# The FFN's remaining GpSimd work goes to VectorE, and sums of the sample's down weights are kept in place

## The chip, the cores and the metric

The kernel runs on one core of a Trainium2 chip. The metric is device time in microseconds of one execution; lower is better.

## The reference

One layer of an encoder with 1024 features, for a prompt of 512 rows and a sample of 1024 rows, in fp32: RMSNorm, an input projection, differential attention beside a recurrent branch, an output projection with residual, then the part that matters here:

```
h2 = rmsnorm(x, norm_ffn)
x  = x + (silu(h2 @ w_gate) * (h2 @ w_up)) @ w_down     # d_ff = 2816
y  = rmsnorm(x, norm_final)
```

## The kernel before

**Split products.** Activations lie feature-major, a page being 128 features by 512 rows. Every fp32 operand of a product is split into a high part (ScalarE casts it to fp32r) and a low part (the operand less its high part, one subtraction of two SBUF tiles). A product is three matmuls a tile: high by high, low by high, high by low (`mm3`, lines 222 to 224). `split` (lines 150 and 151) does the split; `Part.put` (682, 683) does it for a part of the activations, `weight_parts` (713, 714) for FFN weights.

**Stages.** After the prompt's gate and up products and the sample's attention come, in this order:

1. The sample's output projection, then the prompt's low half of the down product (`low_parts` with `down`, 22 steps of 12 matmuls). Beside it `token_parts` normalises the sample's two blocks of 512 rows and forms the parts of the activations that the next stage multiplies. It forms eight sums of 128x1024 by `minus` (line 691).
2. The sample's gate and up (`gate_up`). It treats the two row blocks and the weights as 2 by 2 blocks and does seven products in place of eight (Strassen's scheme in Winograd's form). Each of 11 steps j does gate and up in turn, and each of these forms four sums of weights of 128x512 (lines 706 and 691), splits seven weight parts and multiplies. At the end of a step come the activation, four more sums (`put_sample`, on VectorE already) and seven stores from ScalarE's queue.
3. The sample's down product (`sample_parts`), seven products q = 0 to 6 of 11 steps each, 12 matmuls a step. The weights stay in SBUF as low pages (a11, a12) and high pages (a21, a22). For q = 2 to 5 the weight operand is a sum, made anew in each step in a buffer of the ring "mh", in part on VectorE and in part on GpSimd as FORMS_S says.
4. The prompt's high half of the down product, and the final norms.

**Where GpSimd works.** `minus` has GpSimd as its default; line 706 names it; the low weight split of every third step of `low_parts` goes there (POOL_E); of the sums in stage 3 five instructions a step are its own (one each for q = 2, 3, 4, two for q = 5). Two products in the very last norm are on it in both kernels.

**What sets the order.** Each engine runs its own queue in order. The queues are laid down when the program is built; generators such as `advance` and `Ring` (a look-ahead of five products, LOOK and LOOK2) say which work is put beside which, and a planner places each instruction on its engine's queue when it expects its operands, so that a queue isn't strictly in the order of the code. Loads go out on SP's queue; a raw weight page has three buffers ("raw"), split weights have six ("w").

Of the kernel before, what the change touches and what calls it, by code (L numbers as in the profile page):

```python
# [11 lines left out]
F32 = mybir.dt.float32  # L12
# [4 lines left out]
ALU = mybir.AluOpType  # L17
# [3 lines left out]
P = 128  # L21
# [21 lines left out]
N_RAW, AHEAD, LOOK, LOOK2, LOOK3, LOOK4, LATE = 3, 2, 5, 4, 4, 4, 2  # L43
# [7 lines left out]
SKEW = (0, 1)  # L51
WARM = 16
YG = 0.6
POOL_X = (3,6)

POOL_P = (1, 3, 5)
POOL_S = ()
POOL_E = (0,)
POOL_Q = ()
FORMS_T = (0, 0, 0, 0)  # L60
FORMS_S = (0, 1, 1, 1, 0, 1, 1)
HP_RINGS = ("raw",) * 3 + ("pg",) * 3


# [20 lines left out]
def drain(gen):  # L85
    for _ in gen:
        pass


def build(tc, io, es):  # L90
    nc = tc.nc
    V, A, T = nc.vector, nc.scalar, nc.tensor
    VG = (nc.vector, nc.gpsimd)

    def pool(stack, name, bufs=1, **kw):
        return stack.enter_context(tc.tile_pool(name=name, bufs=bufs, **kw))
# [5 lines left out]
    rings = {}  # L102
# [46 lines left out]
    def split(h, l, src, eng=V):  # L149
        A.copy(h, src)  # L150
        eng.tensor_tensor(l, src, h.bitcast(F32), ALU.subtract)  # L151
# [520 lines left out]
    class Part:  # L672
# [5 lines left out]
        def put(self, src, eng=None):  # L678

            n = 2 * BLK // self.w  # L680
            h, l = (rings[self.ring]([P, n, self.w], self.name + i, F32R) for i in "hl")
            A.copy(h, src)
            (eng or V).tensor_tensor(l, src, h.bitcast(F32), ALU.subtract)
            self.h += [h[:, q] for q in range(n)]
            self.l += [l[:, q] for q in range(n)]

    def parts_of(rs, w):
        return [Part(f"b{i}{w}", r, w) for i, r in enumerate(rs)]

    def minus(out, a, b, eng=nc.gpsimd):  # L690
        eng.tensor_tensor(out, a, b, ALU.subtract)

    def weight_parts(pooled, early=()):

        for j in range(NP):
            for name in ("w_gate", "w_up"):
                r = []
                for f in (j, j + NP):
                    r.append(rings["raw"]([P, KC, P], "wr"))
                    nc.sync.dma_start(r[-1], io[name][f].rearrange("p (k m) -> p k m", k=KC))  # L700
                a11, a12, a21, a22 = (x[:, k:k + 4] for x in r for k in (0, 4))
                s1, s2, s3 = (rings[q]((P, 4, P), f"s{i}") for i, q in enumerate(early or ("mh",) * 3))
                early = ()
                for i, src in enumerate((a11, s2, a12, s3, s1, a22, s2)):
                    if i == 1:
                        nc.gpsimd.tensor_tensor(s1, a21, a22, ALU.add)
                        minus(s2, s1, a11)
                    elif i == 3:
                        minus(s3, a11, a21)
                    elif i == 6:  # L710
                        minus(s2, a12, s2)
                    h = rings["w"]((P, 2, 4, P), "ws", F32R)
                    A.copy(h[:, 0], src)  # L713
                    (nc.gpsimd if i in pooled else V).tensor_tensor(h[:, 1], src, h[:, 0].bitcast(F32), ALU.subtract)
                    yield h[:, 0], h[:, 1]

    def product(out, w, act, first):
# [5 lines left out]
    def pair_products(res, ws, acts, tag, uring, keep):  # L723

        B11, B12, B21, B22, T1, T2, T3, T4 = acts
        n = B11.w
        cost = (3 * ((4 - 1) % FINE + 1)) * n / 2400
        if keep:
            x, y, z = (bank(i, t) for i, t in zip("xyz", tag))
        else:  # L730

            xz, y = bank("xz", tag), bank("y", tag)[:, 0:n]
            x, z = xz[:, 0:n], xz[:, n:2 * n]
        u = rings[uring]([P, 2, n], "u")
        u2, u3 = u[:, 0], u[:, 1]
        e = rings["mh"]([P, 1 if keep else 2, n], "e")
        e, e2 = e[:, 0], e[:, 0 if keep else 1]
        yield from product(x, next(ws), B11, True)
        A.copy(e, x)
        yield cost  # L740
        yield from product(y, next(ws), T2, True)
        V.tensor_tensor(u2, y, e, ALU.add)
        yield cost
        yield from product(x, next(ws), B21, False)
        if not keep:
            A.copy(e2, x)
        yield cost
        yield from product(y, next(ws), T3, False)
        V.tensor_tensor(u3, y, e, ALU.add)
        yield cost  # L750
        yield from product(z, next(ws), T1, True)
        yield cost
        yield from product(y, next(ws), T4, False)
        V.tensor_tensor(u3, z, u3, ALU.add)
        V.tensor_tensor(e, y, e, ALU.add)
        yield cost
        yield from product(z, next(ws), B22, False)
        V.tensor_tensor(u2, z, u2, ALU.add)
        res += [x if keep else e2, u2, e, u3]
        yield cost  # L760

    def gate_up(ws, acts, put, tags, rs, keep):

        n = acts[0].w
        uring, tring = rs
        for j in range(NP):
            gs, us, four = [], [], []
            yield from pair_products(gs, ws, acts, tags[0], uring, keep)
            yield from pair_products(us, ws, acts, tags[1], uring, keep)
            for g, u in zip(gs, us):  # L770
                t = rings[tring]([P, n], "t")
                A.activation(t, g, AF.Tanh, scale=0.5)
                V.scalar_tensor_tensor(t, t, 1.0, g, ALU.add, ALU.mult)
                V.tensor_tensor(t, t, u, ALU.mult)
                four.append(t)
            put(j, four)
# [23 lines left out]
    def low_parts():  # L800

        for f in range(NF):
            hr = rings["xh"](HALF, "hr")
            nc.sync.dma_start(hr, hid[f])
            hp = [rings["mh"](HALF, "hp", F32R) for _ in range(2)]
            split(*hp, hr)
            wr = rings["raw"]([P, KC, P], "wr")[:, 0:4]
            nc.sync.dma_start(wr, io["w_down"][f][:, 0:BLK].rearrange("p (k m) -> p k m", k=4))
            w = rings["w"]((P, 2, 4, P), "ws", F32R)
            split(w[:, 0], w[:, 1], wr, VG[f % 3 in POOL_E])  # L810
            yield (w[:, 0], w[:, 1]), hp

    def down(parts, n, acc, new):
# [115 lines left out]
    b11, b21, b22, t4, t1, t2, t3 = parts_of(["main"] * 4 + ["pg"] * 3, BLK)  # L929
# [50 lines left out]
    def put_sample(j, four):  # L980
        f11, f12, f21, f22 = four
        t1, t2, t4 = (rings["sums"](HALF, f"ht{i}") for i in range(3))
        minus(t1, f12, f11, VG[FORMS_T[0]])
        minus(t2, f22, t1, VG[FORMS_T[1]])
        minus(f12, f22, f12, VG[FORMS_T[2]])
        minus(t4, f21, t2, VG[FORMS_T[3]])
        for q, t in enumerate((f11, f21, t2, t1, f12, f22, t4)):
            nc.scalar.dma_start(hid_s[q][j], t)

    parts = Ring(weight_parts(POOL_S), LOOK)  # L990
    parts.fill()
    drain(gate_up(parts, (b11, None, b21, b22, t1, t2, t3, t4), put_sample, (("aux", "aux", "pv"), ("mm",) * 3), ("pg", "xh"), True))

    low, high = [], []
# [41 lines left out]
    def pair(ring):  # L1039
        w = rings[ring]((P, 2, 4, P), "ws", F32R)  # L1040
        return w[:, 0], w[:, 1]
# [6 lines left out]
    def sample_parts():  # L1048
        loads = Ring(sample_loads(), LOOK4)
        for q in range(7):  # L1050
            for j in range(NP):
                loads.fill()
                a11, a12, a21, a22 = low[j][:, 0], low[j][:, 1], high[j][:, 0] if q else None, high[j][:, 1] if q else None
                if q in (0, 1, 6):
                    src = (a11, a12, a22)[min(q, 2)]
                else:
                    src = rings["mh"]((P, 4, P), "s")
                    if q == 2:
                        VG[FORMS_S[0]].tensor_tensor(src, a21, a22, ALU.add)
                        minus(src, src, a11, VG[FORMS_S[1]])  # L1060
                    elif q == 3:
                        VG[FORMS_S[2]].tensor_tensor(src, a21, a22, ALU.add)
                    elif q == 4:
                        minus(src, a11, a21, VG[FORMS_S[3]])
                    else:
                        VG[FORMS_S[4]].tensor_tensor(src, a11, a12, ALU.add)
                        minus(src, src, a21, VG[FORMS_S[5]])
                        minus(src, src, a22, VG[FORMS_S[6]])
                w = pair("w")
                split(*w, src, VG[q in POOL_Q])  # L1070
                hr = next(loads)
                hp = page()
                split(hp[:, 0], hp[:, 1], hr)
                yield w, (hp[:, 0], hp[:, 1])
# [76 lines left out]
    parts = Ring(sample_parts(), LOOK2)  # L1151
# [83 lines left out]
```

## Time and profile before

| | us |
|---|---|
| median of 3 runs | 1801.11 |
| lowest, highest | 1796.82, 1801.77 |
| the profiled execution's own time | 1798.27 |
| its span, first to last instruction | 1796.5 |

| engine | busy us | share |
|---|---|---|
| TensorE (PE) | 1743.1 | 97% |
| VectorE (DVE) | 1331.4 | 74% |
| ScalarE (ACT) | 827.2 | 46% |
| GpSimd (POOL) | 256.5 | 14% |

Times in the profile's views are microseconds from the span's start. The granted clock of TensorE was 0.989 of full speed over the span. A matmul in flight overlaps the next, so TensorE's busy time can stay near full while fewer matmuls start; their count in a stretch tells more.

### The profile page before, as it was taken

What the parts mean: (1) busy time and instruction counts of PE and PEld (TensorE: products, weight loads), DVE (VectorE), ACT (ScalarE), POOL (GpSimd) and SP (SyncE); (2) the same over time, 40 slices, a digit from 0 to 9 for tenths busy, and PEclk for the clock granted to TensorE, in tenths of its full rate; (3) what the DMA queues carried; (4) which work ended last, traced back from release to release, by engine and by line L of the source; (5) the groups of instructions that cost most, each with busy time, mean ns of one, the idle gap of its engine ahead of it and who ended that gap; (6) DMA issues with size and microseconds to landing.
All of it is one profiled execution on the core that took longest, in us unless ns stands there. A gap on an engine that the chain in (4) does not pass through costs nothing.

```text
span 1796.5 us, 22898 instructions
## 1 busy us (share of the span) xinstructions
PE 1743.1 (97%) x8316; PEld 1434.9 (80%) x8316; DVE 1331.4 (74%) x2154; ACT 827.2 (46%) x1327; POOL 256.5 (14%) x165
## 2 busy tenths in 40 slices
PE   8999999999999999999999979999999999998997
PEld 7777787777888888888788768888888888887797
DVE  6789878777587778786544996767766766989884
ACT  6568556665355545554323432332233334444451
POOL 0000000000000000000000362323322310555200
PEclk9999999999999999999999989999999999999998
DMA  8633424153473222222555642223332239532361
GB/s 291 198 102 111 142 87 135 66 179 119 145 218 114 86 89 93 70 88 71 196 167 180 205 142 100 100 94 106 110 108 100 100 122 369 170 112 70 99 207 54
DMA packets 105026, 238.79 MB, mean 133 GB/s; under 512 B 12240, under 2 KB 21200, under 8 KB 104912
## 3 DMA queue, kind: packets, MB, share of 16 engines
q1 hardware_dynamic: 76608, 185.04, 32.3%
q10 hardware_dynamic: 28304, 52.28, 7.6%
q8 instruction: 65, 1.06, 0.2%
q14 instruction: 49, 0.40, 0.1%
HBM read 180.00 MB, written 57.28 MB: 132 GB/s over the span
## 4 chain that ended last, share of the span: by engine, by line
PE 79%; DVE 10%; ACT 4%; issue 3%; DMA 3%; POOL 1%; ACTq 0%; SPq 0%; DVEq 0%; POOLq 0%
PE gu L222 5%; PE gu L224 4%; PE gu L223 4%; PE pm L223 4%; PE pm L222 4%; PE pm L224 4%; PE acc L223 3%; PE acc L222 3%; PE acc L224 3%; PE y L224 3%; PE y L222 3%; PE y L223 3%; PE sc L591 2%; PE po L223 2%; PE sc L592 2%
## 5 line engine op out<-in xcount | busy, mean ns | idle before, releaser
L222 PE MATMUL pm<-xh,wh 128*128 128x512 f32 x480 | 189.9, 396 | 5.7 <-ACT wh L209 3.3
L223 PE MATMUL pm<-xl,wh 128*128 128x512 f32 x480 | 189.2, 394 | 1.1 <-DVE xl L336 1.1
L224 PE MATMUL pm<-xh,wl 128*128 128x512 f32 x480 | 189.1, 394 | 0.3 <-DVE wl L210 0.3
L209 ACT CAST wh<-wr 128x1024 fp32r<-128x1024 f32 x100 | 104.8, 1048 | 148.5 <-PE gu L223 62.4
L151 POOL TENSOR_TENSOR ws<-wr,ws 128x512 fp32r<-128x512 f32 x8 | 12.7, 1582 | 1013.2 <-ACT ws L150 1013.2
L223 PE MATMUL acc<-hp,ws 128*128 128x512 f32 (+1 forms) x396 | 142.8, 361 | 6.3 <-DVE hp L151 6.3
L222 PE MATMUL acc<-hp,ws 128*128 128x512 f32 (+1 forms) x396 | 143.2, 362 | 2.8 <-ACT hp L150 2.8
L224 PE MATMUL acc<-hp,ws 128*128 128x512 f32 (+1 forms) x396 | 142.5, 360 | 0.6 <-DVE ws L151 0.6
L222 PE MATMUL gu<-yh,wh 128*128 128x512 f32 x352 | 142.0, 403 | 0.9 <-DVE ev L384 0.9
L224 PE MATMUL gu<-yh,wl 128*128 128x512 f32 x352 | 139.0, 395 | 0.0
L223 PE MATMUL gu<-yl,wh 128*128 128x512 f32 x352 | 138.6, 394 | 0.0
L210 DVE TENSOR_TENSOR wl<-wr,wh 128x1024 fp32r<-128x1024 f32 x100 | 122.2, 1222 | 17.6 <-ACT wh L209 16.9
L597 ACT ACTIVATE pb<-pb,mn 128x1024 f32<-128x1024 f32 (+1 forms) x96 | 96.9, 1009 | 73.5 <-DVE mn L594 73.4
L151 DVE TENSOR_TENSOR hp<-hr,hp 128x512 fp32r<-128x512 f32 (+1 forms) x143 | 111.0, 787 | 26.3 <-ACT hp L150 22.4
L594 DVE CUSTOM_DVE_ANT_0 pb<-sc,tab 128x1024 f32<-128x1024 f32 (+1 forms) x96 | 100.1, 1043 | 33.1 <-PE sc L592 31.6
L713 ACT CAST ws<-s 128x512 fp32r<-128x512 f32 x88 | 54.7, 622 | 131.1 <-PE y L224 48.1
L222 PEld LDWEIGHTS pm<-xh,wh 128*128 128x128 f32 x480 | 90.6, 189 | 24.5 <-ACT wh L209 3.5
L150 ACT CAST hp<-hr 128x512 fp32r<-128x512 f32 (+1 forms) x143 | 77.2, 550 | 71.0 <-PE acc L224 24.1
L223 PEld LDWEIGHTS pm<-xl,wh 128*128 128x128 f32 x480 | 90.5, 189 | 19.8 <-DVE xl L336 1.8
L224 PEld LDWEIGHTS pm<-xh,wl 128*128 128x128 f32 x480 | 90.6, 189 | 19.4 <-DVE wl L210 1.0
L713 ACT CAST ws<-wr 128x512 fp32r<-128x512 f32 x66 | 41.1, 622 | 111.1 <-PE y L224 38.2
L223 PEld LDWEIGHTS acc<-hp,ws 128*128 128x128 f32 x396 | 76.3, 193 | 18.1 <-DVE hp L151 7.4
(271 smaller groups left out, 4604.6 us busy)
## 6 DMA issues: line engine op xcount, KB each, us to landing
wr<-w_gate SPq DMA_DIRECT2D x44, 512.0 KB, 3.5
wr<-w_up SPq DMA_DIRECT2D x44, 512.0 KB, 3.5
wr<-w_in SPq DMA_DIRECT2D x40, 512.0 KB, 4.1
hr<-hs SPq DMA_DIRECT2D x77, 256.0 KB, 2.8
hs<-t ACTq DMA_DIRECT2D x44, 256.0 KB, 2.0
hs<-ht ACTq DMA_DIRECT2D x33, 256.0 KB, 2.9
wr<-w_out SPq DMA_DIRECT2D x16, 512.0 KB, 3.6
xd<-xh ACTq DMA_DIRECT2D x28, 256.0 KB, 2.5
```

The source lines that it names most:

```text
L150: A.copy(h, src)
L151: eng.tensor_tensor(l, src, h.bitcast(F32), ALU.subtract)
L209: A.copy(h, r)
L210: V.tensor_tensor(l, r, h.bitcast(F32), ALU.subtract)
L222: T.matmul(out, lhsT=wh, rhs=ah, start=first, stop=False, skip_group_check=more)
L223: T.matmul(out, lhsT=wh, rhs=al, start=False, stop=False, skip_group_check=more)
L224: T.matmul(out, lhsT=wl, rhs=ah, start=False, stop=last, skip_group_check=more)
L591: T.matmul(sc[:, w], lhsT=qh[m][:, qs], rhs=K[m][:, w], start=True, stop=False)
L592: T.matmul(sc[:, w], lhsT=ql[m][:, qs], rhs=K[m][:, w], start=False, stop=True)
L594: V.tensor_tensor_reduce(out=pp[m], in0=sc, in1=tab[:, 896 - q0:896 - q0 + n], scale=-0.125, scalar=3e38, op0=ALU.add, op1=ALU.min, accum_ ...
L597: A.activation(pp[m], pp[m], AF.Exp, scale=-1.0, bias=mn, accum_out=zz)
L713: A.copy(h[:, 0], src)
```

## The change

All FFN sums and splits that GpSimd did are issued on VectorE: the eight sums in `token_parts`, the low splits of `low_parts`, four sums of weights for each gate or up of a step. In the sample's down product the sums are kept: at q = 1 the page a11 is overwritten by a11 - a21, at q = 4 a12 by a12 - a22 and at q = 5 a12 by a12 + a11, so that q = 4 and q = 5 need no buffer of their own, and each of q = 1 to 5 has one sum a step.

```diff
-    def minus(out, a, b, eng=nc.gpsimd):
-        eng.tensor_tensor(out, a, b, ALU.subtract)
+    def minus(out, a, b):
+        V.tensor_tensor(out, a, b, ALU.subtract)
...
-                        nc.gpsimd.tensor_tensor(s1, a21, a22, ALU.add)
+                        V.tensor_tensor(s1, a21, a22, ALU.add)
...
-            split(w[:, 0], w[:, 1], wr, VG[f % 3 in POOL_E])
+            split(w[:, 0], w[:, 1], wr)
...
-                if q in (0, 1, 6):
-                    src = (a11, a12, a22)[min(q, 2)]
-                else:
-                    src = rings["mh"]((P, 4, P), "s")
-                    if q == 2:
-                        VG[FORMS_S[0]].tensor_tensor(src, a21, a22, ALU.add)
-                        minus(src, src, a11, VG[FORMS_S[1]])
-                    elif q == 3:
-                        VG[FORMS_S[2]].tensor_tensor(src, a21, a22, ALU.add)
-                    elif q == 4:
-                        minus(src, a11, a21, VG[FORMS_S[3]])
-                    else:
-                        VG[FORMS_S[4]].tensor_tensor(src, a11, a12, ALU.add)
-                        minus(src, src, a21, VG[FORMS_S[5]])
-                        minus(src, src, a22, VG[FORMS_S[6]])
+                if q == 1:
+                    minus(a11, a11, a21)
+                src = None
+                if q in (2, 3):
                     src = rings["mh"]((P, 4, P), "s")
+                if q == 2:
+                    minus(src, a22, a11)
+                elif q == 3:
+                    V.tensor_tensor(src, a21, a22, ALU.add)
+                elif q == 5:
+                    V.tensor_tensor(a12, a12, a11, ALU.add)
+                if src is None:
+                    src = a11 if q in (0, 4) else a12 if q in (1, 5) else a22
                 w = pair("w")
-                split(*w, src, VG[q in POOL_Q])
+                split(*w, src)
+                if q == 4:
+                    minus(a12, a12, a22)
```

## Rows read from the trace of the kernel before

**Rows 1.** The page: TensorE's busy time; VectorE and GpSimd in 40 slices, tenths.

```profile
PE 1743.1 (97%) x8316; PEld 1434.9 (80%) x8316; DVE 1331.4 (74%) x2154; ACT 827.2 (46%) x1327; POOL 256.5 (14%) x165
...
DVE  6789878777587778786544996767766766989884
...
POOL 0000000000000000000000362323322310555200
```

**Rows 2.** By stretch: length, PE, PEld, DVE, ACT, POOL busy (instructions), clock, DMA, GB/s.

```profile
1016.20:1061.40 45.20, 39.68 (x164) 31.88 (x163) 42.74 (x32) 19.93 (x28) 32.56 (x14) 0.92 0.41 128
1025.00:1050.00 25.00, 20.28 (x80) 16.15 (x79) 25.00 (x18) 12.64 (x19) 15.58 (x6) 0.86 0.40 118
1050.00:1075.00 25.00, 20.41 (x74) 15.54 (x73) 22.84 (x18) 8.44 (x14) 18.65 (x9) 0.86 0.47 166
1075.00:1100.00 25.00, 25.00 (x112) 20.70 (x111) 14.90 (x22) 8.33 (x15) 6.74 (x5) 1.00 0.22 72
1076.00:1474.00 398.00, 396.77 (x1739) 325.24 (x1738) 275.25 (x372) 122.58 (x209) 118.96 (x81) 1.00 0.29 99
1650.00:1675.00 25.00, 16.93 (x61) 12.91 (x61) 21.79 (x26) 12.75 (x24) 15.52 (x10) 0.86 0.23 63
1675.00:1700.00 25.00, 23.48 (x101) 18.74 (x102) 22.41 (x49) 13.26 (x25) 0.00 (x0) 0.93 0.32 100
```

**Rows 3.** TensorE's waits from 975 to 1700 us: total, times, longest.

```profile
PE acc L223 <- DVE hp L151: 6.3, 3, 3.0
PE sc L223 <- DVE hp L151: 4.7, 1, 4.7
```

**Rows 4.** The order of time in the sample's down product: start, duration, instruction.

```profile
1634.70 0.68 DVE L1066 TENSOR_TENSOR s<-wlo 128x512 f32<-128x512 f32 x1
1635.30 0.68 DVE L151 TENSOR_TENSOR ws<-s,ws 128x512 fp32r<-128x512 f32 x1
1635.51 3.32 POOL L691 TENSOR_TENSOR s<-s,whi 128x512 f32<-128x512 f32 x2 [1.29 <-issue]
1635.90 1.79 DVE L151 TENSOR_TENSOR hp<-hr,hp 128x512 fp32r<-128x512 f32 x1
1637.61 1.77 DVE L151 TENSOR_TENSOR ws<-whi,ws 128x512 fp32r<-128x512 f32 x1
```

**Rows 5.** VectorE's groups, 1498 to 1526 and 1016.2 to 1061.4 us: busy, mean ns | idle.

```profile
L151 DVE TENSOR_TENSOR hp<-hr,hp 128x512 fp32r<-128x512 f32 x12 | 8.2, 686 | 3.0 <-ACT hp L150 3.0
...
L659 DVE SCALAR_TENSOR_TENSOR y<-y,par,bc 128x512 f32<-128x512 f32 x8 | 5.4, 744 | 0.2 <-PE bc L271 0.2
L683 DVE TENSOR_TENSOR b4512l<-y,b4512h 128x1024 fp32r<-128x1024 f32 x2 | 2.4, 1213 | 0.0
```

**Rows 6.** The order of time around 990 us, VectorE and TensorE.

```profile
987.49 1.22 DVE L260 TENSOR_TENSOR rtm<-rsm 128x4 f32<-128x4 f32 x1
...
989.66 0.15 DVE L260 TENSOR_TENSOR rtm<-rsm 128x4 f32<-128x4 f32 x1
...
991.27 0.68 PE L271 MATMUL bc<-dg,onesq 128*128 128x128 f32 x4 [3.97 <-DVE dg L270]
```

**Rows 7.** VectorE's groups in the sample's gate and up, 1076 to 1474 us.

```profile
L714 DVE TENSOR_TENSOR ws<-s,ws 128x512 fp32r<-128x512 f32 x82 | 63.1, 769 | 21.1 <-ACT ws L713 19.6
...
L773 DVE SCALAR_TENSOR_TENSOR t<-t,u 128x512 f32<-128x512 f32 x22 | 24.8, 1127 | 0.0
L774 DVE TENSOR_TENSOR t<-t,e 128x512 f32<-128x512 f32 x10 | 17.8, 1777 | 0.0
```

**Rows 8.** ScalarE at the end of a gate and up step, in order of time.

```profile
1110.30 0.59 ACT L739 COPY e<-x 128x512 f32<-128x512 f32 x1 [4.46 <-DVE ht L691]
```

**Rows 9.** GpSimd's first sum of weights, 1076 to 1474 us.

```profile
L706 POOL TENSOR_TENSOR s<-wr 128x512 f32<-128x512 f32 x20 | 27.1, 1356 | 100.9 <-DMA wr<-w_gate 50.9 <-DMA wr<-w_up 50.0
```

**Rows 10.** The last load of a high page's first half, and the use beside which it falls.

```profile
1514.86 0.33 SPq L1009 DMA_DIRECT2D whi<-w_down x1
...
1535.43 1.78 DVE L151 TENSOR_TENSOR ws<-wlo,ws 128x512 fp32r<-128x512 f32 x1
```

More of the change, by code (lines that the diff above doesn't have):

```diff
@@ L53 @@
 YG = 0.6
[L54 to L61, printed above, removed]
 HP_RINGS = ("raw",) * 3 + ("pg",) * 3
@@ L92, in build @@
     V, A, T = nc.vector, nc.scalar, nc.tensor
-    VG = (nc.vector, nc.gpsimd)
     def pool(stack, name, bufs=1, **kw):
@@ L688, in parts_of, with weight_parts @@
         return [Part(f"b{i}{w}", r, w) for i, r in enumerate(rs)]
-    def minus(out, a, b, eng=nc.gpsimd):
-        eng.tensor_tensor(out, a, b, ALU.subtract)
-    def weight_parts(pooled, early=()):
+    def minus(out, a, b):
+        V.tensor_tensor(out, a, b, ALU.subtract)
+    def weight_parts():
         for j in range(NP):
@@ L701, in weight_parts @@
                 a11, a12, a21, a22 = (x[:, k:k + 4] for x in r for k in (0, 4))
-                s1, s2, s3 = (rings[q]((P, 4, P), f"s{i}") for i, q in enumerate(early or ("mh",) * 3))
-                early = ()
+                s1, s2, s3 = (rings["mh"]((P, 4, P), f"s{i}") for i in range(3))
                 for i, src in enumerate((a11, s2, a12, s3, s1, a22, s2)):
                     if i == 1:
-                        nc.gpsimd.tensor_tensor(s1, a21, a22, ALU.add)
+                        V.tensor_tensor(s1, a21, a22, ALU.add)
                         minus(s2, s1, a11)
@@ L713, in weight_parts @@
                     A.copy(h[:, 0], src)
-                    (nc.gpsimd if i in pooled else V).tensor_tensor(h[:, 1], src, h[:, 0].bitcast(F32), ALU.subtract)
+                    V.tensor_tensor(h[:, 1], src, h[:, 0].bitcast(F32), ALU.subtract)
                     yield h[:, 0], h[:, 1]
@@ L982, in put_sample @@
         t1, t2, t4 = (rings["sums"](HALF, f"ht{i}") for i in range(3))
[L983 to L986, printed above, removed]
+        minus(t1, f12, f11)
+        minus(t2, f22, t1)
+        minus(f12, f22, f12)
+        minus(t4, f21, t2)
         for q, t in enumerate((f11, f21, t2, t1, f12, f22, t4)):
             nc.scalar.dma_start(hid_s[q][j], t)
-    parts = Ring(weight_parts(POOL_S), LOOK)
+    parts = Ring(weight_parts(), LOOK)
     parts.fill()
@@ L1052, in sample_parts @@
                 loads.fill()
-                a11, a12, a21, a22 = low[j][:, 0], low[j][:, 1], high[j][:, 0] if q else None, high[j][:, 1] if q else None
-                if q in (0, 1, 6):
-                    src = (a11, a12, a22)[min(q, 2)]
-                else:
-                    src = rings["mh"]((P, 4, P), "s")
-                    if q == 2:
-                        VG[FORMS_S[0]].tensor_tensor(src, a21, a22, ALU.add)
-                        minus(src, src, a11, VG[FORMS_S[1]])
-                    elif q == 3:
-                        VG[FORMS_S[2]].tensor_tensor(src, a21, a22, ALU.add)
-                    elif q == 4:
-                        minus(src, a11, a21, VG[FORMS_S[3]])
-                    else:
-                        VG[FORMS_S[4]].tensor_tensor(src, a11, a12, ALU.add)
-                        minus(src, src, a21, VG[FORMS_S[5]])
-                        minus(src, src, a22, VG[FORMS_S[6]])
+                a11, a12 = low[j][:, 0], low[j][:, 1]
+                a21, a22 = (high[j][:, 0], high[j][:, 1]) if q else (None, None)
+                if q == 1:
+                    minus(a11, a11, a21)
+                src = None
+                if q in (2, 3):
+                    src = rings["mh"]((P, 4, P), "s")
+                if q == 2:
[6 more added lines that the diff above has]
+                    src = a11 if q in (0, 4) else a12 if q in (1, 5) else a22
                 w = pair("w")
-                split(*w, src, VG[q in POOL_Q])
+                split(*w, src)
+                if q == 4:
+                    minus(a12, a12, a22)
                 hr = next(loads)
```

## The prediction

> **What bounds the kernel now.** I read the page first. TensorE is busy for 1743 of 1796.5 us, and GpSimd works only from slice 23 of 40 on (44.9 us each); VectorE is fullest in the slices from 988 to 1078 and 1527 to 1707 us [rows 1]. A share does not say where time is lost, so I next cut the span into stretches and counted matmuls. A full 25 us holds 112 of them, two of which only straddle an edge: one every 25/110 = 0.227 us [rows 2]. Four places fall short, all where GpSimd works:
>
> - A, end of the prompt's low half and start of the sample's gate and up, 1025 to 1075: 80 and 74 matmuls. 70 are missing, 70 x 25/112 = 15.6 us, with the clock at 0.86 [rows 2].
> - B, the first bulk norm, near 987: one wait of 4.0 us for VectorE's diagonal tiles [rows 6].
> - C, the end of the sample's down product, 1650 to 1700: 61 and 101, so 62 missing, 13.8 us [rows 2].
> - G, the sample's gate and up, 1076 to 1474: 398/0.227 + 2 = 1755 would fit and 1739 are there: 16 x 0.227 = 3.6 us [rows 2].
>
> TensorE's waits say for whom: in A and C its longest are for VectorE's low halves, 11.0 us in four waits [rows 3]; the rest of A and C is shorter waits and the matmuls behind them, which run at half pace until the clock is back. So TensorE bounds the kernel, and in A and C VectorE bounds TensorE. Why VectorE is late is seen in order of time [rows 4]: a 128x512 subtraction takes 0.68 us and the next starts 0.60 later, but one issued while a GpSimd sum runs takes 1.77 to 1.79. In that pattern VectorE does four instructions in 1639.3 - 1634.7 = 4.6 us, GpSimd two. Alone, six would take 6 x 0.60 = 3.6. While both read SBUF they take turns, and GpSimd's turn is the longer.
>
> **The change part by part.** Prices: 0.60 us of VectorE's time for a 128x512 instruction (0.69 by itself [rows 4, 5]), 1.14 for 128x1024 (1.21 [rows 5], less the 0.08 by which neighbours overlap), 0.67 for a norm product fed from PSUM (eight in 5.4 us [rows 5]).
>
> *A.* From 1016.2 to 1061.4 VectorE has 45.2 us with 42.7 busy, GpSimd 14 instructions [rows 2]. The same work on VectorE alone: 8 norm products, 5.4; 15 splits of the down step, three of them GpSimd's, 9.0; the first two weight splits and three sums, 3.0; 10 part splits, 11.4; 8 sums of 128x1024, 9.1. That is 37.9, so it ends 7.3 us earlier. The second product of gate and up, which was the first to suffer there, doesn't need the last four of these (two part splits, the fourth part's sum and one weight sum, 4.0 us): it can start at 1061.4 - 7.3 - 4.0 = 1050, or 1052.5 with the 2.5 us that VectorE idled there for ScalarE's casts. TensorE itself would be there at about 1053, eight us earlier than now. The two meet, with no reserve: until then VectorE is still full. All 15.6 us would come back if its order were ideal, 5 if each step is late by a cast as now. I take 11: the two long waits with their slow clock go, some of the small ones stay.
>
> *B.* VectorE's 128x4 product took 1.22 us and the next of its kind 0.15 [rows 6]; the difference is what a turn of GpSimd costs above. About 1 us comes back; bounds 0 and 1.1. The split that moves onto VectorE there (0.60) stands beside other work.
>
> *G.* 81 GpSimd instructions in this stretch [rows 2] become 81 x 0.60 = 48.6 us of VectorE. Waiting for GpSimd goes away: 82 x 0.08 + 22 x 0.44 + 10 x 1.09 = 27 us over 0.69 each [rows 7]. VectorE goes from 275 to about 297 of 398 us, 75%. A quarter idle is cover, but the sums now come in threes, 1.8 us, into one queue with the additions that free TensorE's banks. They fall at the end of a step, where ScalarE's copy of a bank already came 4.5 us late behind a VectorE sum [rows 8] and TensorE lost its 3.6 us. There 1.8 comes in place of 1.1 of waiting: 0.7 more in each of 10 steps would be 7 us. Best case is that the 3.6 us go. I take 3 us lost, between +3.6 won and 8 lost.
>
> A sum also adds a wait: VectorE's first one of each gate or up waits for a weight page. GpSimd stood waiting for these pages 100.9 us in 20 waits [rows 9], 5.0 each, in an otherwise empty queue. On VectorE such a wait would hold up the additions behind it. I cost it at nothing, because split weights are formed five products (5 x 2.7 us) ahead of TensorE, and a planner may put the sum late enough; what it costs otherwise is a rival below.
>
> *C.* The sample's down product has 7 x 11 steps of 12 x 0.227 = 2.72 us on TensorE. VectorE had two splits, plus one sum in q = 2 and 5; GpSimd 55 sums. After: two splits and one sum in q = 1 to 5, 3 x 0.60 = 1.8 us a step, no turn-taking. In q = 5 that replaces a round of 4.6 us, which served one step of q = 5 and a weight split ahead of q = 6 [rows 4] and drained the look-ahead until TensorE stood still after 1649. On VectorE alone but without kept sums, q = 5 would have three sums, 3.0 us a step, over TensorE's 2.72; keeping them is what makes room. I take 13 of the 13.8 us; bounds 8 (residual additions and squares between products still crowd both engines) and 13.8.
>
> The kept sum of q = 1 needs the first half of a21 a whole product earlier. Its last load is issued at 1514.9, and that page's turn on VectorE is near 1535 [rows 10]; 20 us of cover, so nothing. The sums of q = 2 need the second halves as before. What waits behind would be the splits of q = 1. The sum of q = 4 comes after that step's split and feeds a product eleven steps later; 22 buffers of "mh" fewer let loads start earlier. No DMA is added.
>
> A page of the Trainium skill speaks against the change: Perfetto Trace Analysis, section Optimizing Scalar/DVE Operations, says that where VectorE is saturated, giving work to ScalarE or even GpSimd may make sense, and adds that the two share a read port, so that it might not help. By its first half the work should stay where it is and C would get worse, by its second this trace is the case it warns of (1.79 against 0.68 us).
>
> **Sum.** 11 + 1 - 3 + 13 = 22 us. The profiled execution took 1798.3 with 1.8 us around its span; 1798.3 - 22 = 1776. It lies 2.8 below the median of the runs, 1801.1, which would give 1779. I take the middle, 1777.
>
> **The rivals.**
>
> 1. *VectorE stays the limit.* For: it is full in A, and its queue in G gets 22 us more. Against: C has 0.9 us to spare a step. A gives 5, C 8, B 0, G loses 6: 7 us, 1792.
> 2. *All of it comes back.* For: each lost stretch lies where GpSimd works. Against: A meets with no reserve. 15.6 + 13.8 + 1 + 3.6 = 34, or 1766.
> 3. *The weight page holds up VectorE (slower).* In G the first sum stands at the head of VectorE's queue, waiting for its page, and the addition that frees a bank stands behind it; TensorE has one product, 2.7 us, less 0.7 for the addition, before it stops. GpSimd's wait of 5.0 us moved whole would cost 3.0 us, 20 times: 60 us. From 1.25 us a time the other gains (25 us) are spent. At 3.0, 1777 - 3 + 60 = 1834; at half that, 1804. Against: ScalarE's and VectorE's queues in G hold many such loads already, and none shows in TensorE's waits.
> 4. *GpSimd did relieve VectorE (no change).* If the 1.77 us were slow instructions and not turns, what moves to VectorE would cost more than 0.60 each, and C and A gain nothing: 1797 to 1800. Against: the same instruction takes 0.686 on average in a stretch without GpSimd [rows 5].
>
> **How the numbers follow.** Forecast (1771 to 1786) 0.55; rival 1, 0.15; rival 2, 0.15; rival 3, 0.09; rival 4, 0.06. A difference under 0.3% (5.4 us) can't be told from none. Faster: forecast, rivals 1 and 2, less a little where rival 1 ends near 1796: 0.84; same 0.08, from rival 4 and that edge; slower 0.08, rival 3. The range takes in rivals 1 and 2: 1766 to 1793.
>
> **What would show it.** Right: GpSimd near empty; VectorE's 128x512 subtractions at 0.69 everywhere; matmuls per 25 us back near 112 in A and C; no wait of TensorE over 1.5 us after 1649; VectorE near 75% in the gate and up. Wrong: new waits of TensorE for banks in the gate and up, each behind a VectorE sum that waits for a load; gaps at the second product of the gate and up; VectorE waiting for a high page in q = 1. If the time stays within 5 us of before although VectorE's instructions are short again, the premise that its lateness stopped TensorE is wrong.

## The result, and the profile after

The changed kernel takes 1772.4 us (median of 4 runs, 1771.4 to 1773.6), the kernel before 1800.9 in the same comparison: ratio 0.9851, with a 95% interval of 0.9839 to 0.9862. Two later comparisons gave 0.9861 and 0.9863. The profiled execution took 1773.56 with a span of 1771.7, 24.8 us under the span before; by the medians the gain is 28.5.

Busy time in the page of the kernel after, and the 40 slices (each 44.3 us here):

```profile
PE 1733.3 (98%) x8316; PEld 1432.2 (81%) x8316; DVE 1316.5 (74%) x2291; ACT 829.2 (47%) x1327; POOL 1.6 (0%) x6
...
DVE  6789878777578777777453797777777777977784
...
POOL 0000000000000000000000000000000000000000
```

Against [rows 1] VectorE has 137 instructions more and is busy for 15 us less: the waiting in turns that it got rid of outweighs the work that it took over. GpSimd's 256.5 us came down to 1.6.

The stretches of [rows 2] in the kernel after (length, busy time and instructions of PE, PEld, DVE, ACT, POOL, then granted clock, DMA share, GB/s):

```profile
1025.00:1050.00 25.00, 23.84 (x104) 19.02 (x103) 23.89 (x29) 13.31 (x18) 0.00 (x0) 1.00 0.45 141
1050.00:1075.00 25.00, 19.50 (x75) 15.53 (x74) 21.97 (x32) 9.53 (x15) 0.00 (x0) 0.86 0.40 137
1070.00:1460.00 390.00, 390.00 (x1722) 323.08 (x1721) 292.92 (x449) 119.73 (x204) 0.00 (x0) 1.00 0.29 100
1650.00:1675.00 25.00, 24.95 (x116) 20.38 (x116) 18.54 (x42) 11.44 (x21) 0.00 (x0) 1.00 0.16 48
```

Read the counts of matmuls: 112 per 25 us is full. C is full (116; 14 of them are small ones of the norm that follows), and so is the gate and up: 390/0.227 + 2 = 1720. A is still short, by 8 and 37 matmuls, and the clock still falls to 0.86 there.

TensorE's waits from 950 to 1680 us, all there are (total, times, longest):

```profile
PE y L213 <- ACT ws L703: 5.5, 1, 5.5
PE bc L262 <- DVE dg L261: 3.9, 1, 3.9
PE sc L214 <- DVE hp L142: 1.1, 1, 1.1
```

The waits of [rows 3] for low halves of up to 4.7 us are down to 1.1. A new one has come, 5.5 us at the second product of the gate and up, and B's wait has stayed.

Where the time came from, by stage. I took for each kernel the first or last matmul of a stage in the order of time, and the differences are stage times in us:

| stage | before | after | gained | forecast |
|---|---|---|---|---|
| prompt's low half, with the bulk norms (B, most of A) | 77.6 | 71.8 | 5.8 | A 11 + B 1 |
| first three products of gate and up (rest of A) | 16.6 | 16.4 | 0.2 | (in A) |
| rest of gate and up (G) | 415.0 | 410.7 | 4.3 | -3 |
| sample's down product (C) | 227.1 | 212.0 | 15.1 | 13 |
| what follows it | 72.2 | 72.2 | 0 | 0 |

These sum to 25.4; the low half began 0.8 later, which leaves 24.6 of the 24.8.

VectorE's subtractions for the activations in the sample's down product, 1450 to 1680 us, kernel after (busy, mean ns | idle before):

```profile
L142 DVE TENSOR_TENSOR hp<-hr,hp 128x512 fp32r<-128x512 f32 x77 | 52.4, 684 | 1.1 <-ACT hp L141 1.1
```

They are back at 0.684 us, where [rows 4] had 1.77 to 1.79.

### The profile page after: what moved, and what is told of

It reads as the page before. It is cut to its first block, busy times and chain, and to the rows that moved or that the text cites. A ratio compares the mean times of both kernels' runs of the same rounds, so it can differ in the third digit from the quotient of the medians.

```text
span 1771.7 us, 22720 instructions
## 1 busy us (share of the span) xinstructions
PE 1733.3 (98%) x8316; PEld 1432.2 (81%) x8316; DVE 1316.5 (74%) x2291; ACT 829.2 (47%) x1327; POOL 1.6 (0%) x6
## 4 chain that ended last, share of the span: by engine, by line
PE 84%; DVE 6%; DMA 4%; ACT 3%; issue 1%; SPq 0%; DVEq 0%; ACTq 0%
PE pm L213 5%; PE pm L214 5%; PE pm L215 4%; PE gu L213 4%; PE gu L215 4%; PE gu L214 4%; PE acc L215 4%; PE acc L213 4%; PE acc L214 4%; PE y L213 3%; PE y L214 3%; PE y L215 3%; PE z L214 2%; PE z L213 2%; PE z L215 2%; PE x L213 2%
## 5 line engine op out<-in xcount | busy, mean ns | idle before, releaser
L213 PE MATMUL acc<-hp,ws 128*128 128x512 f32 (+1 forms) x396 | 140.9, 356 | 0.0
L215 PE MATMUL acc<-hp,ws 128*128 128x512 f32 (+1 forms) x396 | 140.5, 355 | 0.0
L214 PE MATMUL acc<-hp,ws 128*128 128x512 f32 (+1 forms) x396 | 140.2, 354 | 0.0
L141 ACT CAST hp<-hr 128x512 fp32r<-128x512 f32 (+1 forms) x143 | 77.2, 550 | 54.4 <-PE acc L215 24.6
L142 DVE TENSOR_TENSOR hp<-hr,hp 128x512 fp32r<-128x512 f32 (+1 forms) x143 | 84.6, 603 | 23.7 <-ACT hp L141 20.1
L214 PEld LDWEIGHTS acc<-hp,ws 128*128 128x128 f32 x396 | 75.1, 190 | 10.4
L215 PEld LDWEIGHTS acc<-hp,ws 128*128 128x128 f32 x396 | 75.0, 189 | 10.4
```

Of the source, the lines that this page charges most:

```text
L213: T.matmul(out, lhsT=wh, rhs=ah, start=first, stop=False, skip_group_check=more)
L214: T.matmul(out, lhsT=wh, rhs=al, start=False, stop=False, skip_group_check=more)
L215: T.matmul(out, lhsT=wl, rhs=ah, start=False, stop=last, skip_group_check=more)
```

## The experiments

My theory after the result: VectorE was late because it and GpSimd take turns at two-operand SBUF work, and the turn costs VectorE more than the instruction itself. Rivals: the kept sums (fewer instructions) make the gain in C; or what counts is that GpSimd was slow to hand its results over. For A: VectorE's order, not its total work, now sets the end. The ratios are to the kernel before, run in the same comparison.

| run | median us | ratio [95%] |
|---|---|---|
| e1_down_only | 1783.1 | 0.9911 [0.9896, 0.9926] |
| e2_sums_anew | 1774.1 | 0.9854 [0.9839, 0.9869] |
| e3_idle_gp | 1788.2 | 0.9931 [0.9919, 0.9944] |
| e4_early_sums | 1767.5 | 0.9820 [0.9807, 0.9834] |
| c0_after (the change again) | 1773.3 | 0.9861 [0.9847, 0.9874] |
| e5_weights_gp | 1781.2 | 0.9903 [0.9888, 0.9917] |
| e6_token_gp | 1779.1 | 0.9890 [0.9873, 0.9906] |
| e7_kept_gp | 1785.6 | 0.9927 [0.9914, 0.9940] |
| c1_after (the change again) | 1774.0 | 0.9863 [0.9848, 0.9878] |
| e8_gp_writes | 1772.8 | 0.9854 [0.9839, 0.9868] |
| e9_late_norm | 1770.0 | 0.9840 [0.9825, 0.9854] |
| e10_three_gp | 1775.4 | 0.9874 [0.9857, 0.9890] |

The first four shared a comparison, as did the next four and the last four. c0_after and c1_after are the changed kernel unaltered, as controls:

> The changed kernel again, on the chip of the next three, as what they are compared with: 1771 to 1774.

> The changed kernel again, on the chip of the next three, as what they are compared with: 1771 to 1775.

**e1_down_only: only the sample's down product is changed**, the rest is the kernel before.

```diff
 (sample_parts of the kernel before, with its block replaced by the change's)
-                if q in (0, 1, 6):
...
-                split(*w, src, VG[q in POOL_Q])
+                if q == 1:
+                    minus(a11, a11, a21, V)
...
+                split(*w, src)
+                if q == 4:
+                    minus(a12, a12, a22, V)
```

> Only the sample's down product is changed (kept sums, on VectorE); the weight sums of the gate and up, the token parts and every third low split stay on GpSimd. Theory (turns: VectorE waits out GpSimd's sums that read SBUF, and this lateness stops TensorE): stretch C is a loss of its own, so its 13.8 us come back and nothing else: 1786 to 1789, with the waits around 1036 and 1060 us as before. Rival (backlog: C stops because the look-ahead comes out of the gate and up already drained): 0 to 5 us, 1796 or more.

Measured: 16.5 us under the kernel before, a little more than I expected. The stage takes 212.0, exactly as after, and the low half (77.5) and the gate and up (415.1) stay as before. So C's gain needs nothing from the earlier stages.

**e2_sums_anew: the change, but the down sums made anew in each step, on VectorE.**

```diff
-                if q == 1:
-                    minus(a11, a11, a21)
...
+                    if q == 2:
+                        V.tensor_tensor(src, a21, a22, ALU.add)
+                        minus(src, src, a11)
...
+                    else:
+                        V.tensor_tensor(src, a11, a12, ALU.add)
+                        minus(src, src, a21)
+                        minus(src, src, a22)
```

> The changed kernel, but the sample's down sums are made anew in each step, all on VectorE: two sums a step for q = 2, one for q = 3 and 4, three for q = 5. Theory: it is the turns that cost; without GpSimd q = 5 needs five instructions of 0.60, 3.0 us a step against TensorE's 2.72, 3 us over eleven steps, and a look-ahead of five products takes most of it: 1772 to 1776. Rival (the kept sums are what gains): C is late again, 1780 to 1788.

Measured: 1774.1 against 1773.3 and 1774.0 for the change itself, the stage 212.0. Three sums in each step of q = 5 cost nothing. Keeping the sums is not what gains; taking GpSimd out is.

**e3_idle_gp: the change, and GpSimd makes two sums a step in q = 5 and 6** that go into a page with no further use; VectorE's work is the same.

```diff
+                if q == 6 or q == 5 and j:
+                    for _ in range(2):
+                        nc.gpsimd.tensor_tensor(low[j - 6 + q][:, 0], a21, a22, ALU.add)
```

> The changed kernel with two more GpSimd sums of two SBUF pages in each step of q = 5 and 6 of the sample's down product, written to a page that is dead by then; no later computation uses them. Theory (turns): VectorE's 128x512 subtractions beside them take 1.7 us again; a step of q = 5 costs VectorE up to 1.8 + 2 x 1.1 = 4.0 us and one of q = 6 up to 3.4, against 2.72; 20 us over both, less 13 of look-ahead: 1777 to 1790, with waits of TensorE near the end of q = 5 or in q = 6. Rival (hand-offs: GpSimd was slow to deliver, and its work as such costs nobody): nobody waits for these sums, 1771 to 1774, VectorE at 0.69.

Measured: 1788.2, 14 to 16 us over the three medians of the change. The stage takes 227.2, what it took before (227.1). The group of the idle sums (1587 to 1670 us):

```profile
L1069 POOL TENSOR_TENSOR wlo<-whi 128x512 f32<-128x512 f32 x42 | 67.8, 1626 | 1588.9 <-DVE ws L142 1586.6
```

The same stretch in order of time, and TensorE's wait there:

```profile
1618.67 21.99 POOL L1069 TENSOR_TENSOR wlo<-whi 128x512 f32<-128x512 f32 x13
...
1622.46 1.77 DVE L142 TENSOR_TENSOR hp<-hr,hp 128x512 fp32r<-128x512 f32 x1
1624.16 1.78 DVE L142 TENSOR_TENSOR ws<-wlo,ws 128x512 fp32r<-128x512 f32 x1
```

```profile
PE acc L214 <- DVE hp L142: 9.3, 5, 4.2
```

Here nobody waits for GpSimd's results, so its lateness in handing over is excluded. VectorE starts one subtraction every 1.70 us, GpSimd one sum every 22/13 = 1.69: turns, one for one.

**e8_gp_writes: e3 with a fill in place of each sum**, so that GpSimd writes as much and reads nothing.

```diff
+                        nc.gpsimd.memset(low[j - 6 + q][:, 0], 0.0)
```

> As the kernel with two idle GpSimd sums in each step of q = 5 and 6, but with two GpSimd memsets of 128x512 in their place, which write the dead page and read nothing. Theory (VectorE waits where both read SBUF): the 128x512 subtractions stay at 0.69 and the time at that of the changed kernel, 1771 to 1775. The Trainium skill's page SBUF - State Buffer, section The Big Picture, has the same limit. Rival (any GpSimd instruction on SBUF holds VectorE up): a subtraction takes as long as the memset beside it, 1778 to 1790.

Measured: 1772.8, no different from the change. GpSimd's fills and VectorE's splits (1575 to 1670 us):

```profile
L1069 POOL MEMSET wlo<- 128x512 f32 x42 | 21.8, 526 | 1593.0 <-DVE ws L142 1591.3
...
L142 DVE TENSOR_TENSOR hp<-hr,hp 128x512 fp32r<-128x512 f32 x35 | 23.9, 684 | 0.0
```

And a split with four fills beside it:

```profile
1608.54 0.69 DVE L142 TENSOR_TENSOR hp<-hr,hp 128x512 fp32r<-128x512 f32 x1
1608.68 2.28 POOL L1069 MEMSET wlo<- 128x512 f32 x4 [0.16 <-DVE ws L142]
```

What costs a turn is GpSimd's reading of SBUF, not its writing. The fills were over by 1615 us, while the sums of e3 ran on to 1657, so the total alone would be a weak test; the split at 1608.54 is not. The Trainium skill, SBUF — State Buffer, section SBUF: two separate sides, says that the pair of ports that VectorE and GpSimd share is locked for a whole instruction, and that a VectorE instruction with two SBUF inputs meets that lock only against a GpSimd one that reads SBUF. Both runs agree with it: 1.77 us beside the sums, 0.69 beside the fills. The expectation above names a heading that this page doesn't have; the section meant is this one.

**e6_token_gp: the change, with the eight sums of `token_parts` and the low splits of every third step of `low_parts` back on GpSimd.**

```diff
-            split(w[:, 0], w[:, 1], wr)
+            split(w[:, 0], w[:, 1], wr, V if f % 3 else nc.gpsimd)
...
-            minus(d, hi, lo)
+            nc.gpsimd.tensor_tensor(d, hi, lo, ALU.subtract)
```

> The changed kernel with the eight sums of the token parts and every third low split back on GpSimd. Theory: what A gained comes from here, since VectorE is full there and each GpSimd sum of 128x1024 costs it a turn of 2 us and more: 1776 to 1781. Rival (A's gain comes from the first weight sums): 1771 to 1774.

Measured: 5.8 us slower than c0_after, as expected, 5.3 of it in the low half (77.1 against 71.8 in the profile after; the two repeats of the change show 71.2 and 72.5). The wait of [rows 3] is back, for a split that takes nothing from GpSimd:

```profile
PE sc L214 <- DVE hp L142: 4.7, 1, 4.7
```

**e5_weights_gp: the change, with the four weight sums of each gate or up back on GpSimd.**

```diff
-                        V.tensor_tensor(s1, a21, a22, ALU.add)
-                        minus(s2, s1, a11)
+                        nc.gpsimd.tensor_tensor(s1, a21, a22, ALU.add)
+                        nc.gpsimd.tensor_tensor(s2, s1, a11, ALU.subtract)
```

(and s3 and the second s2 likewise)

> The changed kernel with the four weight sums of each gate or up back on GpSimd. Theory (turns): the end of every step of the gate and up is late again by 0.2 to 0.7 us, 3 us in all, and the first products are late as before: 1775 to 1780. Rival (the prediction's own term for G: sums in threes on VectorE's queue cost 3 us more than the turns): 1768 to 1771.

Measured: 7.8 us slower than c0_after, just above what I expected; 3.5 of it in the rest of the gate and up (414.2), 2.3 in its first three products (18.7). VectorE's two activation instructions, 1070 to 1460 us, are slow again as in [rows 7], and TensorE waits for ScalarE's copies:

```profile
L763 DVE SCALAR_TENSOR_TENSOR t<-t,u 128x512 f32<-128x512 f32 x20 | 24.6, 1228 | 0.0
L764 DVE TENSOR_TENSOR t<-t,e 128x512 f32<-128x512 f32 x10 | 17.8, 1776 | 0.0
```

```profile
PE x L213 <- ACT e L729: 2.5, 4, 1.7
```

The longest of these waits lies in the first three products. So 3.5 of G's 4.3 us are these sums' doing. No run moves them alone, so whether they would gain as much without the rest of the change isn't shown.

**e7_kept_gp: the change, with all five kept sums on GpSimd**, so that VectorE has two splits a step and no sum.

```diff
-                    minus(a11, a11, a21)
+                    nc.gpsimd.tensor_tensor(a11, a11, a21, ALU.subtract)
...
-                    V.tensor_tensor(a12, a12, a11, ALU.add)
+                    nc.gpsimd.tensor_tensor(a12, a12, a11, ALU.add)
```

(and the sums of q = 2, 3 and 4 likewise)

> The changed kernel with the kept sums of the sample's down product on GpSimd, one a step for q = 1 to 5. Theory (turns): VectorE's step is two splits and one turn, 1.2 + 1.1 = 2.3 us, under TensorE's 2.72: 1771 to 1775, although VectorE's subtractions take 1.7 us in places. Rival (hand-offs): every weight operand comes late from GpSimd again, 1778 to 1788.

My theory missed here: 12.3 us slower than c0_after, the stage 223.9, and inside the range of the rival (hand-offs). Its order of time:

```profile
1555.46 1.60 POOL L1057 TENSOR_TENSOR wlo<-wlo 128x512 f32<-128x512 f32 x1
1557.02 1.71 POOL L1063 TENSOR_TENSOR wlo<-wlo,whi 128x512 f32<-128x512 f32 x1
1558.81 1.61 POOL L1057 TENSOR_TENSOR wlo<-wlo 128x512 f32<-128x512 f32 x1
1560.38 1.27 POOL L1053 TENSOR_TENSOR s<-whi,wlo 128x512 f32<-128x512 f32 x1
1561.69 0.62 ACT L141 CAST ws<-s 128x512 fp32r<-128x512 f32 x1 [5.84 <-POOL s L1053]
```

The sums for q = 4 and 5 (L1063, L1057), free of any consumer so early, were laid into GpSimd's queue ahead of the sum that q = 2 needs now (L1053), and ScalarE waits 5.8 us for it. I had reckoned one GpSimd sum a step; here there are three, 4.9 us in a step of 2.7. So a late hand-over does cost time where a backlog stands in GpSimd's own order. How the 12.3 us divide between this and the turns no run shows.

**e10_three_gp: only the sums of q = 1 to 3 on GpSimd**, one a step, with no such backlog.

```diff
-                    minus(src, a22, a11)
+                    nc.gpsimd.tensor_tensor(src, a22, a11, ALU.subtract)
```

(and those of q = 1 and 3)

> The changed kernel with the kept sums of q = 1, 2 and 3 on GpSimd, one a step, and those of q = 4 and 5 on VectorE. With all five on GpSimd the sums of q = 4 and 5 were made early, in the steps of q = 2, and GpSimd had three a step. Theory (turns and GpSimd's own in-order queue, not the hand-off as such): with one a step a VectorE step is 1.2 + 1.1 to 1.2 + 2.2 us where sums of q = 4 and 5 come early on VectorE, near TensorE's 2.72: 1772 to 1779, no wait of TensorE over 2 us in C. Rival (hand-offs): 1780 to 1788.

Measured: 1.3 us over c1_after, the intervals overlapping; TensorE doesn't wait in the stage (212.1). VectorE's splits of the sums still pay, 1500 to 1680 us:

```profile
L142 DVE TENSOR_TENSOR ws<-s,ws 128x512 fp32r<-128x512 f32 x22 | 22.4, 1026 | 0.0
```

So hand-overs without the backlog cost no time that these intervals show. One GpSimd sum a step is carried, because VectorE has room there; the turn is lost but not felt. It becomes time when the look-ahead is used up, as in e3.

**e4_early_sums: the change, with the first weight sums of the gate and up ahead of the last work of the low half.** The last three low pages of the down weights get buffers of the ring "sums", so that the gate's pages can be loaded earlier; the last two parts of the second pair, and the residual additions, go behind the first sums.

```diff
-            wr = rings["raw"]([P, KC, P], "wr")[:, 0:4]
+            wr = rings["sums"]((P, 4, P), "wl") if f >= NF - 3 else rings["raw"]([P, KC, P], "wr")[:, 0:4]
...
+    parts = Ring(weight_parts(), LOOK)
+    parts.fill()
+    lasts(1)
     for m in LO:
```

(`lasts(i)` holds the forming of t4 and b22, which the end of `token_parts` did)

> The changed kernel, but the first weight pages of the sample's gate and up can be loaded earlier (the last three low pages of the down weights go to other buffers), and the first weight sums stand ahead of the last two parts of the activations and of the prompt's residual on VectorE's queue. Theory: in the changed kernel the one long wait left in A, 5.5 us near 1055 and the slow clock behind it, is for the second weight sum, queued behind 6 us of work that TensorE needs later; 6 to 8 us go: 1764 to 1767. Rival: VectorE's total is what limits A, and the wait moves to the parts that are now later: 1769 to 1773.

Measured: 1767.5, 5.8 us under c0_after, with separate intervals, and the fastest of all. It came out just above what I expected; a wait of 2.1 stayed. TensorE's waits, and the first sums:

```profile
PE bc L262 <- DVE dg L261: 4.8, 1, 4.8
PE y L213 <- DVE u L732: 2.1, 1, 2.1
```

```profile
1048.76 0.68 DVE L696 TENSOR_TENSOR s<-wr 128x512 f32<-128x512 f32 x1
...
1053.49 1.23 DVE L674 TENSOR_TENSOR b5512l<-y,b5512h 128x1024 fp32r<-128x1024 f32 x1
```

The sums come ten us earlier, and the first three products take 7.9 us in place of 16.4; 2.4 of this go again at the fourth, which has the wait of 2.1. VectorE does the same work in both kernels: its order, with the loads that allow it, is what A lacked. Earlier loads and the new order are not told apart by a run.

**e9_late_norm: e4, with the bulk norm begun some 14 matmuls later** (YT from 1.5 to 4.0), to give B's chain more time.

```diff
-YT = 1.5
+YT = 4.0
```

> The kernel with the early weight sums, and TensorE's broadcast of the norm's factors (stretch B) placed some 14 matmuls, 3.2 us, later on its queue. Theory: B's wait of 4 to 5 us is TensorE standing in order before a VectorE chain that itself stands behind splits that wait for loads; with other matmuls in front it shrinks by about 3 us, and no GpSimd work has a part in it: 3 to 5 us under the early sums' kernel, 1762 to 1766. Rival: the low products are late for the same loads, so the wait only changes its place: 1766 to 1770.

A miss: 1770.0, no gain over e4, as the rival had it. The wait split up and moved, from 4.8 in one to these three, the longest 2.8:

```profile
PE bc L262 <- DVE dg L261: 4.1, 3, 2.8
```

## Why the prediction was right, and where its terms were off

1777 was forecast, with 1771 to 1786 as its own range; 1772.4 came. That VectorE and GpSimd take turns, and that their absence is the gain, is shown for C by e3 (turns alone, with no result used, cost C's whole gain) and e8 (no turns without reads); in A and G it rests on e6 and e5, which put GpSimd's work back and the loss with it. Not every term was right. A came out about 5 under its forecast and B 1 under, G 7 and C 2 over: that the sum, 22, came near the 25 of the profiles is in part luck. Of the signs of being wrong that I had named one came, the gap at the second product of the gate and up; of the signs of being right one failed, A's matmuls, which stayed at 104 and 75 per 25 us. After 1649 TensorE waits only in the last norms, 2.8 and 1.9 us, as it did before.

*C, 13 forecast, 15.1 measured.* The mechanism held, the size lay over my upper bound of 13.8. The 162 matmuls that I counted from 1650 to 1700 hold 16 small ones of the norm that follows, and I took them for full ones (kernel before, 1650 to 1700 us):

```profile
L271 PE MATMUL bc<-dg,onesq 128*128 128x128 f32 x8 | 1.4, 301 | 0.1
L288 PE MATMUL ss<-onesq,sqd 128*128 128x1 f32 x8 | 0.9, 239 | 0.0
```

Without them 78 are missing, 17.4 us; less the 2.3 that the small ones took, that is the 15.1 measured. All of it was lost in the sixth product (q = 5): by the starts of its matmuls it takes 45.0 us before and 29.9 after, while the other six take the same in both kernels. Wrong, too, was that keeping the sums makes room: e2 has 3.0 us of VectorE a step against TensorE's 2.72 in q = 5 and loses nothing. By an estimate from these numbers 11 such steps lack 3 us, and a look-ahead of five products, 13.6 us, outlasts them.

*A, 11 forecast, about 6 measured.* The failing step is the start of the second product, "1061.4 - 7.3 - 4.0 = 1050, or 1052.5". TensorE was ready for it at 1055.3 (1060.82 less the wait of 5.50), where I had about 1053, but it started at 1060.8. The kernel after in order of time:

```profile
1052.91 1.22 DVE L674 TENSOR_TENSOR b5512l<-y,b5512h 128x1024 fp32r<-128x1024 f32 x1
...
1054.05 0.68 DVE L967 SCALAR_TENSOR_TENSOR xh<-sc,xh 128x512 f32<-128x512 f32 x1
1054.65 1.21 DVE L674 TENSOR_TENSOR b3512l<-y,b3512h 128x1024 fp32r<-128x1024 f32 x1
1055.78 1.22 DVE L674 TENSOR_TENSOR b2512l<-y,b2512h 128x1024 fp32r<-128x1024 f32 x1
1056.91 0.68 DVE L967 SCALAR_TENSOR_TENSOR xh<-sc,xh 128x512 f32<-128x512 f32 x1
1057.52 1.27 DVE L967 SCALAR_TENSOR_TENSOR xh<-acc,xh 128x512 f32<-128x512 f32 x2
1058.71 0.68 DVE L696 TENSOR_TENSOR s<-wr 128x512 f32<-128x512 f32 x1
1059.42 0.69 DVE L682 TENSOR_TENSOR s<-s,wr 128x512 f32<-128x512 f32 x1
1060.15 0.62 ACT L703 CAST ws<-s 128x512 fp32r<-128x512 f32 x1 [0.38 <-DVE s L682]
...
1060.82 0.80 PE L213 MATMUL y<-b5512h,ws 128*128 128x512 f32 x1 [5.50 <-ACT ws L703]
```

The product's last activation part (b5) is done by 1054.1, only some 1.6 us later than I had it. Then stand 4.7 us that it doesn't need: two other part splits, and four residual additions (2.4 us) that my list of VectorE's work left out. Its two weight sums come behind them. I had subtracted the last four instructions as not needed, as if VectorE would pass over them; its queue runs in order. In e4, with the order I had reckoned with, the 5.5 us are gone.

*G, 3 lost forecast, 4.3 gained.* I took the additions at a step's end to pay for the new sums. In the order of time they come ahead of the sums. ScalarE's copy there still waits, though no longer at TensorE's cost:

```profile
1103.18 0.68 DVE L682 TENSOR_TENSOR ht<-t,ht 128x512 f32<-128x512 f32 x1
1103.79 0.68 DVE L696 TENSOR_TENSOR s<-wr 128x512 f32<-128x512 f32 x1
...
1104.32 0.59 ACT L729 COPY e<-x 128x512 f32<-128x512 f32 x1 [4.44 <-DVE ht L682]
```

That is the 4.46 of [rows 8] again, and from the fourth product on TensorE waits nowhere in the stage. In the kernel before, the third product of each later step started 0.1 to 0.7 us late, waiting for this copy. One such start, and one of the slow instructions of [rows 7], which stands ahead of the additions and the copy at 1110.30 (kernel before):

```profile
1102.97 1.78 DVE L774 TENSOR_TENSOR t<-t,e 128x512 f32<-128x512 f32 x1
...
1226.58 0.50 PE L222 MATMUL x<-b1512h,ws 128*128 128x512 f32 x1 [0.51 <-ACT e L739]
```

e5 brings both back, the slow instructions and the late starts, 0.1 to 0.5 us in ten steps; no run holds the slow instructions apart from the rest of GpSimd's work there. VectorE is busy for 292.9 of 390 us, the 75% forecast. One of the groups that were slow (kernel after, 1070 to 1460 us):

```profile
L763 DVE SCALAR_TENSOR_TENSOR t<-t,u 128x512 f32<-128x512 f32 x20 | 13.8, 688 | 0.0
```

*B, 1 forecast, nothing measured.* The product of [rows 6] that took 1.22 us is short now, and the wait is as long as it was (3.9 against 3.97):

```profile
987.55 0.15 DVE L251 TENSOR_TENSOR rtm<-rsm 128x4 f32<-128x4 f32 x1
987.62 0.68 DVE L142 TENSOR_TENSOR ws<-wr,ws 128x512 fp32r<-128x512 f32 x1
...
991.69 0.62 ACT L141 CAST ws<-wr 128x512 fp32r<-128x512 f32 x1 [1.42 <-DMA wr<-w_down]
992.34 0.69 DVE L142 TENSOR_TENSOR ws<-wr,ws 128x512 fp32r<-128x512 f32 x1 [1.27 <-ACT ws L141]
992.95 0.15 DVE L253 SCALAR_TENSOR_TENSOR rsm<-rtm,rsm 128x4 f32<-128x4 f32 x1
...
993.58 0.69 PE L262 MATMUL bc<-dg,onesq 128*128 128x128 f32 x4 [3.90 <-DVE dg L261]
```

The split that moved onto VectorE (987.62) stands in this chain and not beside it, as I had thought. The chain's last link stands in VectorE's queue behind a split whose page ScalarE had to wait for. That this load sets the end now is read from these rows alone; e9 moved the norm and the wait moved along, which doesn't settle it. So what held B stays open.

*The rivals.* Rival 3 (a weight page holds up VectorE) didn't come. VectorE's first sums of weights over the whole run, idle time before them 0.0 against GpSimd's 100.9 in [rows 9]:

```profile
L696 DVE TENSOR_TENSOR s<-wr 128x512 f32<-128x512 f32 x22 | 15.0, 683 | 0.0
```

Each sum stands behind other work, and its page was there when its turn came. In A the sums' place behind other work cost the 5.5 us. Rival 4 (GpSimd did relieve VectorE) is excluded by e3, and rival 1 by C and G, though A gave little more than the 5 us that it had there. Of rival 2's 34 us some 25 came; e4 fetches 6 more.

## What to carry to other kernels

A GpSimd instruction that reads SBUF isn't free help beside a busy VectorE: price it by what VectorE's two-operand instructions take beside it (here 1.1 us more each, for a sum that VectorE does in 0.60). When an engine's total falls, look next at its order: walk its queue up to the instruction that the critical engine needs, and count everything ahead of it, needed or not. When matmuls are counted to find lost time, leave the small ones out: 16 of them hid 1.3 us of the loss here. And when a forecast sum comes out near, check it term by term.

## What the runs showed of the hardware

GpSimd filled a 128x512 fp32 tile in 0.526 us without lengthening VectorE's subtractions beside it (0.684 on average, e8), while its sum of the same size took 1.63 us in turns with VectorE (e3; 1.27 where VectorE left it alone, e7) and brought the subtraction to 1.77. I had not expected sums that nobody uses to cost as much as the sums that were needed: 227.2 and 227.1 us for the stage. The two kernels place different numbers of such sums, 42 and 55, so that the times agree so closely is not explained by any run.
